# MLP of a two-sample encoder in two passes: Strassen's form in the first layer, the middle kept in DRAM

## The chip, the cores and the metric

The kernel runs on one core of a Trainium2 chip. The metric is device time in microseconds (us), of one execution of the whole program. The engines are PE (TensorE, matrix products into PSUM), DVE (VectorE), ACT (ScalarE), POOL (GpSimd) and SP (SyncE, which issues nearly all transfers).

## What is computed

Two samples of 1024 tokens and 1024 features go through one encoder layer: attention and a state-space mixer side by side, an output projection, an MLP with 4096 hidden columns, and a gate with a side input. The part that the change is about:

```python
    mix = jnp.concatenate([rms_norm(att, g_att_out), rms_norm(ssm, g_ssm_out)], axis=-1)
    h = h + mix @ w_out
    f = rms_norm(h, g_mlp)
    h = h + jnp.square(jax.nn.relu(f @ w_mlp1)) @ w_mlp2
    e = rms_norm(h, g_ple)
    h = h + jax.nn.sigmoid(e @ w_ple_gate) * (p_i @ w_ple_proj)
    ...
    return rms_norm(h, g_final)
```

All of it is fp32. The kernel writes each fp32 operand as a sum of two rounded parts, `hi` and `lo` (a cast on ACT, then a subtraction, "the split"), and a product takes three matmuls: hi·hi, lo·hi and hi·lo (`mm3`, L460 to L463).

## The kernel before

The program has three phases. A (to about 588 us) norms the input, multiplies by `w_in` and runs the state-space part. B (588 to 940 us) is attention together with the gated unit of the mixer (`Glu`, L976); there the order on PE, ACT and DVE is written out by hand in steps, and `GLU_LATE` says how many steps the gated unit starts late. Its tile `yt` is loaded at L1001, squared on POOL (L1005) and taken up by DVE at L1008. C (`PhaseC`, L1149) does the rest, first for sample 0 (943 to 1870 us), then for sample 1 (to 2757 us). In C the order of instructions on each engine is set by a scheduler, which follows the order of the program text where operands and buffers allow and fills gaps with later work.

For one sample C does this. `W_out` is multiplied in two halves of 512 tokens, each added to `h`, which stays in SBUF as eight tiles (L1312). After each half, `norm` makes the normalized rows: squares on ACT, a reciprocal root by Newton's steps on DVE (L419 to L428), a scaled copy `ft` (L556), and per token tile eight transposes on PE into `n_ps` (L561), whose results are split into `acth` and `actl` (L449, L450). Then come eight chunks of 512 hidden columns. Layer 1 of a chunk is a plain product: 4 blocks of 128 columns by 2 token halves by 8 steps of contraction, each three matmuls; POOL splits the weights (L1184), ACT applies relu and square (L1334, L1335), and the tile `hid` stays in SBUF. Layer 2 of the chunk adds `hid` times 512 rows of `w_mlp2` to `h`. It has Strassen's form with seven products p1 to p7 (here run in the order p1, p2, p6, p5, p3, p7, p4): the token halves by the two halves of 256 of the contraction on the left (`hid`), two halves of the contraction by two column halves of 512 on the right (`wr_b`). Sums of the right side are made on POOL (L1217), of the left on DVE (L1222 to L1228), both as 128x1024; each operand is split before its product, the right side on POOL, the left on DVE (both L1184), with three buffers of each kind (`ops`). `into_h` adds the products to `h` (L1270) and to a running sum `u2` (L1279) as they leave PSUM. The last chunk's layer 2 is plain, with the norm for the gate between its halves. The scheduler mixes layer 2 of one chunk with layer 1 of the next on PE. For sample 0, one or two tiles of sample 1's attention output are normed within each chunk (`AttNorm`, L1085), with tiles from the pool `raw`, which also holds layer 1's weights as they land (`w`).

Of the kernel before, what the change touches and what calls it, by code (L numbers as in the profile page):

```python
# [16 lines left out]
P = 128  # L17
# [482 lines left out]
GLU_LATE = 3  # L500
# [475 lines left out]
class Glu:  # L976
# [15 lines left out]
    def gelu(self):  # L992
# [155 lines left out]

class PhaseC:  # L1149
    def __init__(self, nc, tc, ctx, bp, a0, io, ident, scr):  # L1150
        self.nc, self.tc, self.io, self.ident, self.scr = nc, tc, io, ident, scr
        self.bp = bp
# [6 lines left out]
        self.actp = [a0, pool("a", 4)]  # L1159
        self.hp = pool("h", 1)  # L1160
        self.raw = pool("raw", 3)
        self.wp = pool("w", 8)
# [3 lines left out]
        self.pm2 = pool("p2", 5, space=PSUM)  # L1166

# [5 lines left out]
    def norm(self, h, gb, a, i):  # L1173

        a.half(i)
# [11 lines left out]
    def product(self, a, b, ts=range(4)):  # L1187

        nc = self.nc
        banks = {t: self.pm2.tile([P, 512], F32, tag="m2", name="m2") for t in ts}  # L1190
# [15 lines left out]
    def strassen(self, A, s1, B, t2, read, end=(range(4),)):  # L1206

        nc = self.nc
        v, g = nc.vector, nc.gpsimd
# [4 lines left out]
        read(1, self.product([A[0, 0]], B[0, 0]))  # L1218
        each(B[0, 0], B[0, 1], B[0, 0])
        each(t2, B[1, 1], B[0, 0])  # L1220
        read(2, self.product([A[0, 1]], B[1, 0]))
# [357 lines left out]
```

## Time and profile before

| | |
|---|---|
| three runs | 2756.2, 2758.74, 2759.26 us; median 2758.74 |
| the profiled execution | 2758.93 us, with a span of 2757.2 us |
| granted TensorE clock, mean | 0.972 of full speed |
| busy share of the span | PE 93%, DVE 59%, ACT 41%, POOL 41% |

A row of the trace is an instruction, or several alike: start, duration, engine and line, operation, output<-inputs, shapes, and in brackets how long the engine had been idle before it and what released it. Matmuls are pipelined, so a row's duration is longer than the distance to the next one. Windows give the busy time of each engine in a stretch; the stretches used here are the chunks of sample 1 and the layer part of each sample.

### The profile page before, as it was taken

The page shows a single profiled execution, that of the slowest core. Times are in us where ns is not written, and L with a number is a line of the kernel's source. Part 1 is how long each engine was busy: PE and PEld are TensorE (multiplying, and loading weights), DVE is VectorE, ACT ScalarE, POOL GpSimd, SP SyncE. Part 2 cuts the span into 40 slices and gives each one's busy share as a digit, 9 for nine tenths or more (in the row PEclk, how much of TensorE's full clock was granted, in tenths as well). Part 3 has the DMA queues.
Part 4 walks back from the last instruction along what each step waited for, and adds up shares of the span by engine and source line. Part 5 has one row for each costly group of instructions (what it writes and reads, how often), then busy time and mean ns, then how long its engine had stood idle before and what let it go on. Part 6 is the DMA issues. An engine that isn't in the chain of part 4 may idle for free.

```text
span 2757.2 us, 33930 instructions
## 1 busy us (share of the span) xinstructions
PE 2568.5 (93%) x12206; PEld 2040.7 (74%) x12206; DVE 1631.9 (59%) x2891; ACT 1139.8 (41%) x2282; POOL 1138.5 (41%) x819
## 2 busy tenths in 40 slices
PE   5998888969998899999999999999999999999997
PEld 4866666756555677788888878787788888888786
DVE  4788786457766534565555673655355554467455
ACT  6433323327657534333333434443433333333442
POOL 2133234223331243545544653445445555455442
PEclk9999998989999999999999999999999999999999
DMA  8534453355346800221212221262111111111111
GB/s 271 156 85 115 158 177 96 109 162 155 123 135 223 271 31 27 73 73 45 67 46 62 73 88 46 85 224 86 54 54 51 38 58 61 54 54 52 60 39 62
DMA packets 267145, 268.74 MB, mean 97 GB/s; under 512 B 41808, under 2 KB 216912, under 8 KB 264928
## 3 DMA queue, kind: packets, MB, share of 16 engines
q1 hardware_dynamic: 265888, 266.44, 30.5%
q8 instruction: 96, 1.57, 0.2%
q14 instruction: 73, 0.60, 0.1%
q0 software_dynamic: 1088, 0.14, 0.1%
HBM read 196.63 MB, written 67.66 MB: 96 GB/s over the span
## 4 chain that ended last, share of the span: by engine, by line
PE 75%; DVE 14%; DMA 4%; ACT 3%; issue 2%; POOL 1%; SPq 0%; DVEq 0%; ACTq 0%; POOLq 0%
PE m L461 19%; PE m L462 19%; PE m L463 19%; PE ag L462 2%; PE ag L461 2%; PE ag L463 2%; PE glu L1033 2%; PE pss L804 1%; PE pt L844 1%; PE po L865 1%; DMA w<-in_w_mlp_dram 1%; ACT sb L836 1%; PE s_pb L251 1%; PE n_ps L561 1%; DVE s_t L274 1%
## 5 line engine op out<-in xcount | busy, mean ns | idle before, releaser
L1184 POOL TENSOR_TENSOR lo<-wr_b,hi 128x512 fp32r<-128x512 f32 x264 | 381.4, 1452 | 554.1 <-ACT hi L1183 522.7
L461 PE MATMUL m<-acth,hi 128*128 128x512 f32 x1024 | 398.8, 391 | 3.5 <-ACT hi L1183 3.5
L462 PE MATMUL m<-acth,lo 128*128 128x512 f32 x1024 | 399.4, 390 | 1.8 <-POOL lo L1184 1.8
L463 PE MATMUL m<-actl,hi 128*128 128x512 f32 x1024 | 398.4, 390 | 0.0
L1270 DVE TENSOR_TENSOR h<-h,m 128x512 f32<-128x512 f32 x448 | 288.1, 680 | 132.2 <-PE m L463 132.1
L462 PE MATMUL m<-hi,lo 128*128 128x512 f32 x912 | 354.3, 391 | 3.9 <-DVE lo L1184 3.5
L463 PE MATMUL m<-lo,hi 128*128 128x512 f32 x912 | 351.1, 390 | 0.1
L1183 ACT CAST hi<-wr_b 128x512 fp32r<-128x512 f32 x264 | 163.9, 621 | 444.4 <-PE m L462 416.0
L461 PE MATMUL m<-hi 128*128 128x512 f32 x912 | 335.6, 394 | 5.3 <-DVE h L1270 4.1
L1184 DVE TENSOR_TENSOR lo<-hid,hi 128x512 fp32r<-128x512 f32 x200 | 188.2, 942 | 146.3 <-ACT hi L1183 146.2
L1184 POOL TENSOR_TENSOR lo<-w,hi 128x512 fp32r<-128x512 f32 x128 | 176.0, 1382 | 161.4 <-ACT hi L1183 159.1
L461 PEld LDWEIGHTS m<-acth,hi 128*128 128x128 f32 x1024 | 192.3, 188 | 45.2 <-ACT hi L1183 5.1
L462 PEld LDWEIGHTS m<-acth,lo 128*128 128x128 f32 x1024 | 192.7, 188 | 43.7 <-POOL lo L1184 3.9
L463 PEld LDWEIGHTS m<-actl,hi 128*128 128x128 f32 x1024 | 192.4, 188 | 40.2 <-DVE actl L450 0.4
L461 PE MATMUL m<-hi,acth 128*128 128x512 f32 x512 | 201.2, 394 | 5.2 <-DVE h L1312 2.6
L461 PEld LDWEIGHTS m<-hi 128*128 128x128 f32 x912 | 170.9, 188 | 44.3 <-DVE h L1270 7.8
L462 PEld LDWEIGHTS m<-hi,lo 128*128 128x128 f32 x912 | 171.5, 188 | 42.3 <-DVE lo L1184 7.3
L462 PE MATMUL m<-hi,actl 128*128 128x512 f32 x512 | 201.0, 393 | 0.0
L463 PEld LDWEIGHTS m<-lo,hi 128*128 128x128 f32 x912 | 171.5, 188 | 36.4 <-POOL lo L1184 0.9
L463 PE MATMUL m<-lo,acth 128*128 128x512 f32 x512 | 191.3, 393 | 2.3 <-POOL lo L1184 2.3
L1334 ACT ACTIVATE hid<-m 128x512 f32<-128x512 f32 x128 | 76.1, 595 | 218.7 <-PE m L463 217.4
L461 PE MATMUL ag<-acth,whi 128*128 128x512 f32 x384 | 155.3, 406 | 3.6 <-ACT acth L546 3.6
(354 smaller groups left out, 4929.7 us busy)
## 6 DMA issues: line engine op xcount, KB each, us to landing
w<-in_w_mlp_dram SPq DMA_DIRECT2D x128, 256.0 KB, 2.9
wr_b<-in_w_mlp_dram SPq DMA_DIRECT2D x32, 1024.0 KB, 4.9
wraw<-in_w_in_dram SPq DMA_DIRECT2D x32, 512.0 KB, 4.9
out_dram<-h SPq DMA_DIRECT2D x16, 512.0 KB, 2.7
mixa<-ato SPq DMA_DIRECT2D x24, 256.0 KB, 2.5
v<-zv SPq DMA_DIRECT2D x8, 576.0 KB, 6.5
xt<-in_x_sample_dram SPq DMA_DIRECT2D x8, 512.0 KB, 8.2
xt<-in_x_prompt_dram SPq DMA_DIRECT2D x8, 512.0 KB, 5.7
```

The source lines that it names most:

```text
L251: nc.tensor.matmul(pb[:, k], w[:, i, g + k], u[:, g + k], start=True, stop=True)
L274: v.tensor_tensor_scan(flat(dst)[64:128, 0:n - 1][:, ::-1], flat(r0)[64:128, 0:n - 1][:, ::-1], flat(src)[64:128, 1:n][:, ::-1], 0.0, op0= ...
L461: nc.tensor.matmul(out, l[0], r[0], start=first, stop=False)
L462: nc.tensor.matmul(out, l[1], r[0], start=False, stop=False)
L463: nc.tensor.matmul(out, l[0], r[1], start=False, stop=last)
L561: nc.tensor.transpose(pt[:, i], dst[:, P * k:P * k + P], ident)
L804: self.nc.tensor.matmul(pss[h][:, u, w], ql, kr, start=True, stop=True)
L1033: nc.tensor.matmul(o, self.w[:, k, P * f:P * f + P], gt[k][:, c], start=k == 0, stop=k == 3)
L1183: self.nc.scalar.copy(hi, src)
L1184: lo_eng.tensor_tensor(lo, src, hi.bitcast(F32), op=ALU.subtract)
L1270: eng.tensor_tensor(o, o, x, op=ALU.add)
L1334: nc.scalar.activation(z, o, AF.Relu)
```

## The change

Layer 1 gets Strassen's form. A chunk of 512 hidden columns is a 2x2 problem: two halves of 256 hidden columns (weights, left) by two halves of 512 of the contraction by two halves of 512 tokens (right). The seven right sides are three of the normalized quarters, B11, B21 and B22, and four sums T0 to T3. All stay in SBUF, split, for the whole pass: they are made once per sample by the class `Sums`, tile by tile within the norm of the second token half, from the transposes in PSUM and from the first half rebuilt as `f` = hi + lo on POOL. Per token tile DVE makes two differences and the `lo` of two, POOL two differences and the `lo` of two, and ACT five casts. A chunk is then 7 products of 24 matmuls. The results go through relu and square and are stored to DRAM (`hid`); so is `h`, which is loaded again for the second pass.

Layer 2 runs afterwards as a pass of its own: three Strassen groups of 1024 of the contraction (seven products of 48 matmuls, which gather twice the contraction in PSUM), then chunk 6 in the form of 256 and chunk 7 as before. A group loads eight operands of 1 MB into single places. All SBUF of C is divided into 16 places `K(i)`, whose use is rotated from one sample to the next. Operand sums are made in pieces of 128x1024, those of the right side all on POOL (L1264 for both engines), and the products alternate between two PSUM pools. The attention norm of sample 1 moves to chunks 1 to 7 of layer 1. `GLU_LATE` goes from 3 to 5, and the first two loads of `yt` get a higher priority.

The diff, cut to what the prediction speaks of:

```diff
-GLU_LATE = 3
+GLU_LATE = 5
...
-                nc.sync.dma_start(out=yt, in_=scr["y"][8 * f:8 * f + 8, :, :, s].rearrange("g h t c -> (g h) t c"))
+                with B.tc.high_priority(offset=FIRST_AHEAD if s == 0 and f < 2 else 0):
+                    nc.sync.dma_start(out=yt, in_=scr["y"][8 * f:8 * f + 8, :, :, s].rearrange("g h t c -> (g h) t c"))
...
+class Sums:
+    def __init__(self, B, f11, f21, tile, raw):
+        self.B, self.f11, self.f21, self.raw = B, f11, f21, raw
+        self.T = [[tile(i, x) for x in "hl"] for i in range(4)]
+
+    def put(self, nc, kq, T, ps):
+        v, g = nc.vector, nc.gpsimd
+        c = slice(P * (T % 4), P * (T % 4) + P)
+
+        def sum_(i, e, x, y):
+            f = self.raw.tile([P, 4, P], F32, tag="raw", name=f"f{i}")
+            e.tensor_tensor(f, x, y, op=ALU.subtract)
+            hi, lo = (x[:, :, c] for x in self.T[i])
+            nc.scalar.copy(hi, f)
+            e.tensor_tensor(lo, f, hi.bitcast(F32), op=ALU.subtract)
+            return f
+        if kq == 0:
+            self.f1 = sum_(0, v, ps, self.f11[:, :, c])
+            return
+        f2 = sum_(1, v, ps, self.f1)
+        last = self.B.put(nc, kq, T, ps)
+        sum_(2, g, f2, self.f11[:, :, c])
+        sum_(3, g, self.f21[:, :, c], f2)
+        return last
...
-        self.wp = pool("w", 8)
+        self.wp = pool("w", 4)
...
-        def each(out, x, y):
-            for i, (o, p, q) in enumerate(zip(out, x, y)):
-                (v if i else g).tensor_tensor(o, p, q, op=ALU.subtract)
+        def op(e, out, x, y, how=ALU.subtract):
+            for k in range(0, out.shape[1], 2):
+                e.tensor_tensor(*(z[:, k:k + 2] for z in (out, x, y)), op=how)
+        product(1, A[0, 0], B[0, 0])
+        op(g, B[0, 0], B[0, 1], B[0, 0])
+        op(g, t2, B[1, 1], B[0, 0])
+        product(2, A[0, 1], B[1, 0])
+        op(v, s1, A[1, 0], A[1, 1], ALU.add)
+        op(v, A[1, 0], A[0, 0], A[1, 0])
+        op(v, A[0, 0], s1, A[0, 0])
+        op(g, B[0, 1], B[1, 1], B[0, 1])
+        product(6, A[0, 0], t2)
+        op(g, B[1, 0], B[1, 0], t2)
+        op(v, A[0, 1], A[0, 1], A[0, 0])
+        product(5, s1, B[0, 0])
...
+    def layer1(self, ch, o, hid, norm=None):
...
+        def done(i, l, banks, x):
+            z = self.t2.tile([P, 2, 512], F32, tag="t2", name="z")
+            add(z, x, banks)
+            nc.scalar.activation(z, z, AF.Relu)
+            nc.scalar.activation(z, z, AF.Square)
+            nc.sync.dma_start(out=hid[l, :, i], in_=z.rearrange("p f c -> p (f c)"))
...
+        p1 = product(A[0, 0], B11)
+        for f in range(2):
+            nc.scalar.copy(u[:, f], p1[f])
+        done(0, 0, product(A[0, 1], B21), u)
+        if norm:
+            norm()
...
+        f = [K(R[6 + kq], [4, 512], F32, "f") for kq in range(2)]
+        for kq in range(2):
+            nc.gpsimd.tensor_tensor(f[kq], fa.hi[kq, 0].bitcast(F32), fa.lo[kq, 0].bitcast(F32), op=ALU.add)
...
+        for c in range(3):
+            A, b = {}, {}
+            for j, l, pa_, pb_ in ((0, 0, 6, 2), (1, 0, 7, 3), (0, 1, 8, 4), (1, 1, 9, 5)):
+                A[l, j] = K(R[pa_], [4, 512], F32, "hid")
+                nc.sync.dma_start(out=A[l, j].rearrange("p k c -> p (k c)"),
+                                  in_=scr["hid", s, 2 * c + j][l].rearrange("p i c -> p (i c)"))
```

The order that this gives is shown at two places. First POOL, at the start of a layer 2. Before, `wr_b` are operands of `w_mlp2`, `t` is a sum, and `w` are weights of the next chunk's layer 1:

```order
L1184 TENSOR_TENSOR lo<-wr_b_12378,hi 128x512 x2
L1184 TENSOR_TENSOR lo<-wr_b_12380,hi 128x512
L1217 TENSOR_TENSOR wr_b_12378<-wr_b_12378 128x2x512
L1184 TENSOR_TENSOR lo<-w_12312,hi 128x512
L1217 TENSOR_TENSOR t_12382<-wr_b_12380,wr_b_12378 128x1024
L1217 TENSOR_TENSOR wr_b_12378<-wr_b_12380,wr_b_12378 128x2x512
L1184 TENSOR_TENSOR lo<-w_12318,hi 128x512
L1184 TENSOR_TENSOR lo<-wr_b_12380,hi 128x512
L1217 TENSOR_TENSOR wr_b_12380<-wr_b_12380,t_12382 128x2x512
L1184 TENSOR_TENSOR lo<-t_12382,hi 128x512
```

And now, at the start of a group (`wr` are the operands of `w_mlp2`, `t2` the sum):

```order
L1229 TENSOR_TENSOR lo_12132<-wr_12107,hi_12131 128x512
L1229 TENSOR_TENSOR lo_12152<-wr_12107,hi_12151 128x512
L1264 TENSOR_TENSOR wr_12107<-wr_12115,wr_12107 128x1024
L1229 TENSOR_TENSOR lo_12172<-wr_12107,hi_12171 128x512
L1264 TENSOR_TENSOR t2_12122<-wr_12119,wr_12107 128x1024
L1264 TENSOR_TENSOR wr_12115<-wr_12119,wr_12115 128x1024
L1229 TENSOR_TENSOR lo_12192<-wr_12107,hi_12191 128x512
L1229 TENSOR_TENSOR lo_12228<-wr_12111,hi_12227 128x512
L1229 TENSOR_TENSOR lo_12248<-wr_12111,hi_12247 128x512
L1264 TENSOR_TENSOR wr_12107<-wr_12115,wr_12107 128x1024
L1264 TENSOR_TENSOR wr_12111<-wr_12111,t2_12122 128x1024
L1229 TENSOR_TENSOR lo_12268<-wr_12111,hi_12267 128x512
```

Twice as many sums stand between the splits of the first two products, in pieces, and no splits of layer 1 among them. The second place is PE behind `W_out`, in the norm of the second token half. Before (sample 1), `m` here is the first product of layer 2, which runs between the transposes of `n_ps`:

```order
L561 MATMUL n_ps<-ident,ft 128x128 x12
L461 MATMUL m_16229<-hi 128x512
L461 MATMUL m_16230<-hi 128x512
L461 MATMUL m_16231<-hi 128x512
L461 MATMUL m_16232<-hi 128x512
L462 MATMUL m_16229<-hi,lo 128x512
L463 MATMUL m_16229<-lo,hi 128x512
L462 MATMUL m_16230<-hi,lo 128x512
L463 MATMUL m_16230<-lo,hi 128x512
L462 MATMUL m_16231<-hi,lo 128x512
L463 MATMUL m_16231<-lo,hi 128x512
L462 MATMUL m_16232<-hi,lo 128x512
```

After 20 more transposes layer 1 follows there. Now (`mz` are PSUM banks of layer 1, `acth` and `actl` right sides of the first token half, `Th` and `Tl` sums, `B` the quarter B22):

```order
L461 MATMUL mz<-acth,hi 128x512
L462 MATMUL mz<-acth,lo 128x512
L463 MATMUL mz<-actl,hi 128x512
L561 MATMUL n_ps<-ident,ft 128x128 x32
L461 MATMUL mz<-Th,hi 128x512 x4
L461 MATMUL mz<-B_15931,hi 128x512
L462 MATMUL mz<-B_15931,lo 128x512
L461 MATMUL mz<-B_15931,hi 128x512
L462 MATMUL mz<-B_15931,lo 128x512
L462 MATMUL mz<-Th,lo 128x512
```

Ahead of the transposes stand only the rest of the two products that need the first token half alone, and behind them come products that need the second. POOL at the same place (`f` are the rebuilt quarters and the differences):

```order
L1229 TENSOR_TENSOR lo<-w_15941,hi 128x512
L1229 TENSOR_TENSOR lo<-w_15943,hi 128x512
L1438 TENSOR_TENSOR f<-acth,actl 128x2048 x2
L1165 TENSOR_TENSOR f_16077<-f_16071,f 128x512
L1165 TENSOR_TENSOR f_16081<-f,f_16071 128x512
L1168 TENSOR_TENSOR Tl<-f_16077,Th 128x4x128
L1168 TENSOR_TENSOR Tl<-f_16081,Th 128x4x128
L1165 TENSOR_TENSOR f_16106<-f_16100,f 128x512
L1165 TENSOR_TENSOR f_16110<-f,f_16100 128x512
L1168 TENSOR_TENSOR Tl<-f_16106,Th 128x4x128
L1168 TENSOR_TENSOR Tl<-f_16110,Th 128x4x128
L1165 TENSOR_TENSOR f_16135<-f_16129,f 128x512
```

The four operations per token tile stand in tile order, behind the two rebuilt quarters.

## Rows read from the trace of the kernel before

**Rows 1.** Page part 1: engine, busy us (share of the span), instructions

```profile
PE 2568.5 (93%) x12206; PEld 2040.7 (74%) x12206; DVE 1631.9 (59%) x2891; ACT 1139.8 (41%) x2282; POOL 1138.5 (41%) x819
```

**Rows 2.** Windows, one of four: busy us (count) of PE, PEld, DVE, ACT, POOL, clock, DMA share

```profile
2143.20:2224.80 81.60, 81.60 (x362) 67.59 (x360) 43.60 (x59) 30.30 (x53) 41.82 (x27) 1.00 0.17 52
```

**Rows 3.** Windows of the layer part, first and second sample

```profile
1066.60:1755.80 689.20, 675.38 (x2975) 551.18 (x2975) 402.22 (x590) 269.15 (x474) 335.24 (x211) 1.00 0.21 63
1977.60:2643.60 666.00, 663.72 (x2945) 548.57 (x2944) 358.39 (x486) 258.76 (x450) 329.59 (x211) 1.00 0.17 55
```

**Rows 4.** Timeline of PE at 999: start, us, engine, line, operation

```profile
998.77 0.39 PE L462 MATMUL m<-hi,actl 128*128 128x512 f32 x1
...
1000.81 0.39 PE L462 MATMUL m<-hi,actl 128*128 128x512 f32 x1
```

**Rows 5.** Groups by shape, 2143.2 to 2469.6: busy us, mean ns, idle before

```profile
L1184 POOL TENSOR_TENSOR lo<-wr_b,hi 128x512 fp32r<-128x512 f32 x49 | 71.8, 1471 | 97.4 <-ACT hi L1183 94.0 <-DMA wr_b<-in_w_mlp_dram 3.4
...
L1184 DVE TENSOR_TENSOR lo<-hid,hi 128x512 fp32r<-128x512 f32 x48 | 43.5, 905 | 40.0 <-ACT hi L1183 40.0
...
L1279 DVE TENSOR_TENSOR u<-u,m 128x512 f32<-128x512 f32 x32 | 20.7, 676 | 0.0
...
L1217 POOL TENSOR_TENSOR wr_b<-wr_b 128x1024 f32<-128x1024 f32 x4 | 9.6, 2403 | 0.0
...
L1222 DVE TENSOR_TENSOR s<-hid 128x1024 f32<-128x1024 f32 x4 | 5.0, 1260 | 59.0 <-ACT hid L1335 59.0
```

**Rows 6.** Timeline of POOL, 2168 to 2186

```profile
2169.75 1.29 POOL L1184 TENSOR_TENSOR lo<-w,hi 128x512 fp32r<-128x512 f32 x1 [1.43 <-ACT hi L1183]
...
2174.62 2.83 POOL L1217 TENSOR_TENSOR wr_b<-wr_b,t 128x1024 f32<-128x1024 f32 x1
2177.40 2.29 POOL L1184 TENSOR_TENSOR lo<-t,hi 128x512 fp32r<-128x512 f32 x1
```

**Rows 7.** Timeline of DVE, 2168 to 2186

```profile
2174.50 0.68 DVE L1184 TENSOR_TENSOR lo<-hid,hi 128x512 fp32r<-128x512 f32 x1
...
2176.30 2.23 DVE L1224 TENSOR_TENSOR hid<-s,hid 128x1024 f32<-128x1024 f32 x1
```

**Rows 8.** Windows, behind W_out of the second sample

```profile
1951.70:1977.70 26.00, 19.96 (x96) 15.23 (x94) 21.63 (x33) 14.83 (x28) 13.75 (x7) 0.97 0.07 20
```

**Rows 9.** Timeline of PE, first transposes of that norm

```profile
1963.79 1.82 PE L561 MATMUL n_ps<-ident,ft 128*128 128x128 f32 x12 [0.18 <-DVE ft L556]
```

**Rows 10.** Timeline of DVE, 1950 to 1980

```profile
1957.14 2.32 DVE L420 TENSOR_SCALAR nr<-na 128x4 int32<-128x4 int32 x1
...
1962.36 2.48 DVE L556 SCALAR_TENSOR_TENSOR ft<-h,nr,gbc 128x1024 f32<-128x1024 f32 x2
```

**Rows 11.** Timeline of POOL, 1950 to 1980

```profile
1957.03 2.40 POOL L1217 TENSOR_TENSOR wr_b<-wr_b,wr_b 128x1024 f32<-128x1024 f32 x1
```

**Rows 12.** Timeline of PE in attention, 600 to 623

```profile
599.64 1.13 PE L804 MATMUL pss<-k,q 64*128 64x256 f32 x8
...
620.25 1.09 PE L844 MATMUL pt<-ident,sb 128*128 128x128 f32 x4 [18.46 <-DVE pT L848]
```

**Rows 13.** Timeline of PE in attention, 620 to 628

```profile
622.85 2.08 PE L804 MATMUL pss<-k,q 64*128 64x256 f32 x8
```

**Rows 14.** Waits of SP's queue, 938 to 2757: total us, times, longest

```profile
SPq L1100 <- ACT ato L1097: 286.6, 8, 42.8
```

**Rows 15.** Timeline of DVE in attention, 596 to 623

```profile
615.32 2.90 DVE L1008 SCALAR_TENSOR_TENSOR ge<-ge,yt 128x1024 f32<-128x1024 f32 x1 [17.88 <-POOL ge L1005]
```

**Rows 16.** Timeline of POOL in attention, 596 to 623

```profile
613.40 3.74 POOL L1005 TENSOR_TENSOR ge<-yt 128x1024 f32<-128x1024 f32 x2 [34.37 <-DMA yt<-y_scr]
```

**Rows 17.** Timeline of PE at the second sample's start

```profile
1879.89 0.50 PE L461 MATMUL m<-hi,acth 128*128 128x512 f32 x1 [2.60 <-DVE h L1312]
```

**Rows 18.** Page part 6: transfers, count, KB each, us to landing

```profile
wr_b<-in_w_mlp_dram SPq DMA_DIRECT2D x32, 1024.0 KB, 4.9
```

More of the change, by code (lines that the diff above doesn't have):

```diff
@@ L1166, in __init__, with places, tile, half @@
         self.pm2 = pool("p2", 5, space=PSUM)
+        self.R = list(range(16))
+    @staticmethod
+    def places(bp, a0, kp=None):
+        def tile(i, shape, dt, name):
+            pool = a0 if i < 4 else bp if 8 <= i < 12 else kp
+            return pool.tile([P] + shape, dt, tag=f"k{i}", name=name, bufs=1)
+        return tile
+    def half(self, a, th, ids):
+        for kq in range(2):
+            a.hi[kq, th], a.lo[kq, th] = (self.K(i, [4, 512], F32R, "act" + x) for i, x in zip(ids[2 * kq:2 * kq + 2], "hl"))
+        return a
     def gvec(self, src, n):
@@ L1185, in split, with product @@
         return hi, lo
-    def product(self, a, b, ts=range(4)):
+    def product(self, a, b, odd=False):
         nc = self.nc
-        banks = {t: self.pm2.tile([P, 512], F32, tag="m2", name="m2") for t in ts}
+        ts = range(4)
+        banks = {t: (self.pm1 if odd and t < 3 else self.pm2).tile([P, 512], F32, tag="m1" if odd and t < 3 else "m2", name="m2")
+                 for t in ts}
         b = [x[:, k] for x in b for k in range(x.shape[1])]
@@ new lines, in rows, with mixed @@
+    @staticmethod
+    def rows(nc, w, r0, K, i):
+        t = K(i, [2, D], F32, "wr")
+        nc.sync.dma_start(out=t, in_=w[r0:r0 + 2 * P].rearrange("(k p) c -> p k c", p=P))
+        return [t[:, :, 512 * l:512 * l + 512] for l in range(2)]
+    @staticmethod
+    def mixed(nc, K, ids, scr, s, th):
+        A = Act(None, ())
+        for kq, nm in enumerate(("mixa", "ssm")):
+            for i, d in enumerate((A.hi, A.lo)):
+                d[kq, th] = t = K(ids[2 * kq + i], [4, 512], F32R, "mix")
+                nc.sync.dma_start(out=t.bitcast(F32), in_=scr[nm, s][i, :, :, 512 * th:512 * th + 512].rearrange("f p c -> p f c"))
+        A.th = th
+        return A
@@ new lines, in run @@
+                self.norm(h, gb, self.half(fa, 0, R[0:4]), 0)
+        f = [K(R[6 + kq], [4, 512], F32, "f") for kq in range(2)]
+        for kq in range(2):
+            nc.gpsimd.tensor_tensor(f[kq], fa.hi[kq, 0].bitcast(F32), fa.lo[kq, 0].bitcast(F32), op=ALU.add)
+        fa.hi[1, 1], fa.lo[1, 1] = (K(R[4 + i], [4, 512], F32R, "B22") for i in range(2))
+        o = Sums(fa, f[0], f[1], lambda i, x: K(R[8 + 2 * i + "hl".index(x)], [4, 512], F32R, "T" + x), self.raw)
+        for ch in range(8):
+            self.layer1(ch, o, scr["hid", s, ch], None if ch else lambda: self.norm(h, gb, o, 1))
+            if s == 0 and ch > 0:
+                if ch == 1:
+                    N = AttNorm(nc, self.raw, "raw", self.sm, pm1, "m1", ident, self.gvec(io["g_att_out"], 512), io, scr)
+                for T in range(ch - 1, ch + ch // 7):
+                    N.run(1, T, 1)
```

227 lines of the change are left out of this document (119 added, 108 removed).

## The prediction

> **What bounds the kernel now.** I read the busy table first: TensorE works 93% of the span [rows 1]. That is a mean over stages, so the second look is at the stretch that the change rewrites, in windows. Of the second sample's eight chunks, four windows of 81.6 us were taken, and in each of them PE has no idle time at all, while POOL is busy for about half and DVE a little more [rows 2]. The whole layer stretch of that sample is idle on PE for 666.0 - 663.7 = 2.3 us. The first sample's is longer, 689.2 us, with 689.2 - 675.4 = 13.8 us of idle PE [rows 3]. So the MLP is bounded by the number of matmuls, and each matmul removed is worth its own issue time as long as nothing else comes late. A row gives 0.39 us to a 512-wide matmul, but they are pipelined: from 998.77 to 1000.81 there are nine steps, 0.2267 us each [rows 4]. What stands beside PE is read from the shapes in the same stretch [rows 5].
>
> **The matmuls removed.** Layer 1 of one chunk is 4 blocks x 2 token halves x 8 contraction steps x 3 = 192 matmuls now, and 7 products x 24 = 168 in the new form. Layer 2 keeps its count: a group of 1024 is 7 x 48 = 336, and the two chunks that it stands for were 2 x 7 x 24. Saved: 24 x 8 chunks x 2 samples = 384, times 0.2267 = **-87.1 us**. In the order, the 512-wide rows of this arithmetic fall from 9072 to 8688, which is the same 384.
>
> **Layer 1 after.** POOL has 14 splits of 128x512 per chunk where it had 8 and, in layer 2, its sums besides. At the price of an undisturbed one, 1.29 us [rows 6], that is 18.1 us against PE's 168 x 0.2267 = 38.1. DVE has 14 additions with a PSUM operand at 0.68 [rows 5] and four sums at 1.26, 14.6 us in all. Both fit with room, so I cost nothing here; if they did not, each product would wait for its last split.
>
> **The fronts of layer 2.** Before, the additions that make Strassen's operands lie under the next chunk's layer 1, whose 192 matmuls the scheduler mixes in. In the second pass nothing is left to mix in. One contraction step is 12 matmuls, 2.72 us. In a group, the first three products (p1, p2, p6) need nearly all sums: from the first split that three buffers allow, two steps ahead, to the last step of p6 there are 13 steps = 35.4 us. In that time POOL must do 12 splits and 8 sums, 12 x 1.29 + 8 x 2.40 [rows 5, 6] = 34.7 us, which just fits; DVE must do 12 splits at 0.68 [rows 7] and 6 sums at 1.26 [rows 5], 15.7 us. What decides is whether these overlap. In the trace they don't: DVE's L1224 starts at 2176.30 inside POOL's 2.83 us and takes 2.23 instead of 1.26; it ends at 2178.53, just over 1 us after POOL's at 2177.45; POOL's next split, 2177.40, then takes 2.29 instead of 1.29 [rows 5 to 7]. Additions with a PSUM operand stay at 0.68 throughout [rows 5]. Serial work would be 50.4 us; successive starts lie some 0.06 closer than the durations say (2174.62 to 2177.40 is 2.78, the row has 2.83), so with 38 operations about 48, and the group loses 13 us. If POOL alone set the pace it would lose 0. I take 10, nearer the serial end, which is what the rows look like. The first group of a sample can do three sums early, under the last layer-1 chunk, when its weights have landed: 10 - 7 = 3 (bounds 0 and 8). Chunk 6, still of 256, has half the splits and sums: serial 25.2 in 19.0 us, so 6 at most, and I take 4. Per sample 10 + 10 + 3 + 4 = 27, **+54 us** for both, between 0 and 2 x (13 + 13 + 8 + 6) = 80. Behind the front the rest of a group has 16 splits on each engine and two sums on DVE, 34 us of work under 43.5 us of PE, and loses nothing.
>
> The Trainium skill says of this pair (SBUF — State Buffer, "Who interferes with whom") that the port VectorE and GpSimd share is an exclusive lock, not a division of bandwidth. The trace agrees in the 2.23 and 2.29 us just read. Taken strictly it speaks against this change, since it moves all of the right-hand sums to POOL and takes their cover away; the sum by it alone is the first rival's, and by POOL's own time alone the second's.
>
> **The norm of the second token half.** Its matmul stream is thin already: in the 26.0 us behind W_out, PE works 19.96 [rows 8], so 6.0 us are idle. It fills the wait with layer 1 and the first product of layer 2; the first transposes start at 1963.79 [rows 9], 12.1 us after the window's start. Now p1 and p2 of chunk 0 leave 42 matmuls, 9.5 us, and all other products need sums over all four token tiles. Two things are added. First, POOL rebuilds f, twice 128x2048, as soon as W_out has ended; no row shows this shape, I take twice the 2.40 of 128x1024, 4.8 each. Newton's steps on DVE come just then: L420, four columns, took 2.32 under a POOL sum of 2.40 [rows 10, 11]. So the transposes start 0 to 4.4 us later. Second, each tile costs POOL four operations, 5.2 us, and DVE an L556 (1.24 each in the pair of 2.48 [rows 10]) and two splits; serial 7.8 a tile. With three buffers, the next tile's second difference waits for the third of POOL's four. The last T1 part is then ready 4.5 + 2.75 tiles after the first transposes: at 12.1 + 4.5 + 14.3 = 31 or at 16.5 + 4.5 + 21.5 = 42.5 us. PE has 9.5 us of products and some 5 of transposes in it, so it idles 16.5 to 28, less the 6.0 of before: +10.5 to +22. I take +16 per sample, the middle, as f and the lock each may or may not hit: **+32 us**.
>
> **The clock behind a hole.** After 18.46 us without work on PE, eight score matmuls took 2.08 us where the same eight had taken 1.13 just before it [rows 12, 13]: half speed, some 4 us lost. The holes at the norm become longer than 6 us, so I add 2 per sample, **+4** (0 to 8).
>
> **What gets cheaper.** (1) Attention's norm in the first sample shares three raw buffers with the first layer's weights; SP stands 286.6 us at L1100 behind it [rows 14]. The weights get buffers of their own, and of the 13.8 - 2.3 = 11.5 us extra idle PE I take **-9** (0 to -11.5). (2) In attention, DVE waits 17.88 us at L1008 for POOL, POOL for the load of yt [rows 15, 16], and PE 18.46 behind it [rows 12]. The order shows the two loads at the same place on SP as before in spite of the priority, but DVE's operation two steps later, with two score groups and two pT copies ahead of it that used to be behind: **-6** (0 to -12). If the load is what limits, the wait just stays for the later one. (3) At the second sample's start PE waits 2.60 us for an addition to h [rows 17]; h now comes in pairs and earlier, **-2.6** (0 at worst). (4) The additions to h fall to four sevenths, since a group does the work of two chunks; they were under PE, so nothing. Hidden values (32 MB) and h (8 MB) are stored to DRAM and loaded again; 1 MB lands in 4.9 us [rows 18], and a group's 8 MB are spread over 76 us. Nothing in the forecast, but it is a rival.
>
> **Sum**, against the profiled execution's 2758.9 us (the median of the runs shown is 2758.7, the same for this purpose): -87.1 - 9 - 6 - 2.6 + 54 + 32 + 4 = -14.7, so **2744 us**.
>
> **The rivals.** *All port work serial (slower).* Every front pays 13, the first groups 8, chunk 6 pays 6, the norms +22 and 8 for the clock: 80 + 44 + 8 = 132 against 104.7 gained, 2786 us. For it: every overlap in [rows 6, 7] is serial. Against: DVE's sums can slide into gaps when POOL waits for a cast. It decides as soon as fronts, norms and clock pass 110 us together. *POOL alone sets the pace (much faster).* DVE's splits fall between POOL's, fronts cost some 6 per sample, norms +10 each, clock 2: 104.7 - 34 = 71, 2688 us. For it: POOL's own 34.7 us fits in 35.4, and POOL idles half of the layer stretch now [rows 3]. Against: the lock. *The round trip through DRAM comes late.* Each of the eight starts (three groups and chunk 6, two samples) waits one landing of 4.9 for its last operand, since a place is free only when the last product has split it: +40 on the forecast, 2784 us. For it: one place per operand. Against: these places come free three steps before the group ends, and nothing before p2 and the sum s1 needs the last ones. *The load of yt doesn't move*: 2750 us; it is inside the forecast's own range.
>
> **How the numbers follow.** Forecast 0.50, in its own range 2722 to 2766 (about 0.36 faster, 0.11 within, 0.03 slower); serial 0.25, slower; POOL alone 0.15, faster; late loads 0.10, nearly all slower. By over 0.2% (5.5 us, about what a measurement of this kernel can tell from no change): faster 0.52, same 0.12, slower 0.36. The range reaches 2695 to 2790, so that about half of the POOL-alone case and the dearest serial ones stay out.
>
> **What would show it.** In the new profile layer-1 chunks should take 38.1 us of solid PE and middle groups 76.2 plus the front's loss, with PE released by POOL's or DVE's splits in p1 to p6. PE idle in the 30 to 45 us behind W_out should be 16 to 28 us, released by T sums. L1009 on DVE should wait less than 17.9 us. The prediction is wrong in its main step if middle groups run at 76 to 79 us (no lock), or if PE waits there for loads; and in its second if the norm's hole stays near 6 us.

## The result and the profile after

The changed kernel takes 2826.8 us (median of four runs, 2825.7 to 2829.1) against 2758.0: a ratio of 1.0251, with an interval of 1.0233 to 1.0269. It is slower by 69 us, where 15 us less were forecast, and outside the range. The profiled execution has a span of 2824.7 us and a mean granted clock of 0.948 (0.972 before). In the rows of this kernel L461 to L463 are still the three matmuls; a split is L1229, an operand sum of layer 2 L1264, the differences of `Sums` L1165 and their `lo` L1168, the rebuilt `f` L1438, an addition to `h` L1386, and the sums of layer 1's own weights L1361 to L1364.

Page part 1 (engine, busy us, share of the span, instructions), beside [rows 1]:

```profile
PE 2531.4 (90%) x11822; PEld 1996.8 (71%) x11822; DVE 1850.0 (65%) x2963; ACT 1210.5 (43%) x2306; POOL 1357.2 (48%) x951
```

PE has its 384 matmuls less, but only 37 us less of busy time where these matmuls were worth 87, and the span grew by 67.5. So PE idles 105 us more than before, and its mean clock is lower: the time is in PE's waits and in slow matmuls behind them. PE's waits from 930 us to the end (engine, tile, line <- what released it: total us, times, longest):

```profile
PE m L462 <- DVE lo L1229: 73.6, 41, 5.5
PE n_ps L561 <- DVE B L450: 19.7, 4, 5.7
PE mz L461 <- ACT Th L1167: 16.2, 2, 8.1
PE n_ps L561 <- DVE ft L556: 8.3, 4, 3.4
PE m L461 <- DVE h L1386: 7.5, 13, 0.7
PE n_ps L573 <- DVE att L570: 5.4, 1, 5.4
PE n_ps L561 <- DVE f L1165: 5.0, 4, 1.4
```

The first line is layer 2 waiting for a split of a left side; the second, third and seventh are the norm of the second token half; the sixth is the last tile of `AttNorm`. The stages of the second sample, in windows (from:to, length, then busy us and counts of PE, PEld, DVE, ACT, POOL, the clock, DMA share, GB/s): layer 1, the norm ahead of it, the three groups, and the rest to the end.

```profile
2015.80:2311.80 296.00, 296.00 (x1295) 244.87 (x1296) 121.21 (x143) 133.53 (x184) 157.84 (x115) 0.99 0.43 145
1974.30:2015.80 41.50, 17.47 (x76) 13.39 (x74) 34.64 (x44) 19.02 (x35) 30.93 (x15) 0.69 0.20 76
...
2312.00:2403.50 91.50, 81.20 (x335) 65.04 (x334) 73.39 (x68) 37.31 (x63) 63.07 (x37) 0.94 0.35 122
2403.50:2497.20 93.70, 82.32 (x331) 65.76 (x331) 76.57 (x76) 32.49 (x56) 62.12 (x36) 0.93 0.23 84
2497.20:2590.10 92.90, 82.18 (x335) 65.61 (x335) 82.14 (x78) 32.27 (x56) 64.62 (x36) 0.93 0.31 112
2590.10:2824.70 234.60, 210.74 (x932) 169.38 (x930) 160.00 (x253) 92.62 (x166) 114.29 (x75) 0.96 0.09 33
```

Layer 1 is what was forecast: 1296 matmuls without a gap. At the 0.2267 of [rows 4] that is 293.8 us, and it has 296.0. The groups are not: 336 matmuls are 76.2 us at that pace, and the three take 15.3, 17.5 and 16.7 more. Where does one of them lose it? PE in the middle one (start, us, engine, line, ..., in brackets the idle time before and its releaser):

```profile
2409.46 1.07 PE L461 MATMUL m<-hi 128*128 128x512 f32 x4
...
2420.75 2.07 PE L462 MATMUL m<-hi,lo 128*128 128x512 f32 x4 [5.50 <-DVE lo L1229]
2422.63 1.54 PE L463 MATMUL m<-lo,hi 128*128 128x512 f32 x4
2426.82 0.65 PE L462 MATMUL m<-hi,lo 128*128 128x512 f32 x1 [2.65 <-DVE lo L1229]
```

DVE in the same stretch:

```profile
2408.39 2.89 DVE L1229 TENSOR_TENSOR lo<-hid,hi 128x512 fp32r<-128x512 f32 x1
2411.20 3.41 DVE L1264 TENSOR_TENSOR s<-hid 128x1024 f32<-128x1024 f32 x1
2414.53 4.50 DVE L1264 TENSOR_TENSOR hid<-hid 128x1024 f32<-128x1024 f32 x2
2418.95 1.75 DVE L1229 TENSOR_TENSOR lo<-hid,hi 128x512 fp32r<-128x512 f32 x1
2420.62 3.39 DVE L1264 TENSOR_TENSOR hid<-s,hid 128x1024 f32<-128x1024 f32 x1
2423.93 2.83 DVE L1229 TENSOR_TENSOR lo<-hid,hi 128x512 fp32r<-128x512 f32 x1
```

And POOL:

```profile
2407.34 3.39 POOL L1264 TENSOR_TENSOR t<-wr 128x1024 f32<-128x1024 f32 x1
2410.68 2.84 POOL L1264 TENSOR_TENSOR wr<-wr 128x1024 f32<-128x1024 f32 x1
2413.49 6.66 POOL L1229 TENSOR_TENSOR lo<-wr,hi 128x512 fp32r<-128x512 f32 x3
2420.11 2.81 POOL L1264 TENSOR_TENSOR wr<-wr 128x1024 f32<-128x1024 f32 x1
2422.89 3.32 POOL L1264 TENSOR_TENSOR wr<-wr,t 128x1024 f32<-128x1024 f32 x1
```

Read the last two together. Both engines are busy without a pause, and each operation of one lasts until one of the other is through: a sum on DVE is 2.2 to 3.4 us where it was 1.26 alone, a split 1.75 to 2.89 where it was 0.68; POOL's three splits take 6.66 where 3.87 would do. And DVE works in order. PE needs the split that begins at 2418.95; ahead of it stand three sums for later products, from 2411.20 on. PE gets it at 2420.7 and runs the next matmuls at half pace: four in 2.07 us, where four took 1.07 at 2409. The granted clock of that stretch is 0.50, the lower of its two levels (1.2 GHz, where full speed is 2.4):

```profile
2420.70:2423.50 2.80, 2.75 (x7) 2.17 (x8) 2.80 (x1) 0.58 (x1) 2.80 (x2) 0.50 0.00 0
```

Over the three groups of this sample the distances between PE's starts give some 37 us of waits, and some 60 starts that lie 0.42 apart instead of 0.227, 12 us.

The first group has hardly a head start. Its operands are asked for late (SP's queue near the end of layer 1):

```profile
2295.68 0.80 SPq L1460 DMA_DIRECT2D hid<-hid  x2
2301.12 0.93 SPq L1464 DMA_DIRECT2D wr<-in_w_mlp_dram  x2
```

The load of 2301.12 took 8.3 us to land. DVE's first sum starts at 2307.31 and POOL's at 2309.75, with layer 1 done at 2312.0.

In the norm PE idles 41.5 - 17.5 = 24.0 us, at a clock of 0.69, against 6.0 in [rows 8]. From `W_out`'s first half (in the second sample, from behind the wait of [rows 17]) to the 600th matmul of 512 columns behind it, PE takes 19.8 us longer than before, in both samples. POOL's rebuilt `f` and two of its pairs of differences there:

```profile
1974.30 9.18 POOL L1438 TENSOR_TENSOR f<-acth,actl 128x2048 f32<-128x2048 f32 x2 [0.71 <-PE m L462]
1992.14 4.61 POOL L1165 TENSOR_TENSOR f<-f,f 128x512 f32<-128x512 f32 x2 [8.66 <-DVE f L1165]
1996.71 2.50 POOL L1168 TENSOR_TENSOR Tl<-f,Th 128x512 fp32r<-128x512 f32 x2
1999.29 3.80 POOL L1165 TENSOR_TENSOR f<-f,f 128x512 f32<-128x512 f32 x2
2003.05 3.92 POOL L1168 TENSOR_TENSOR Tl<-f,Th 128x512 fp32r<-128x512 f32 x2
```

DVE, which L420 holds up under the first of them, and which has four more operations that the forecast didn't count:

```profile
1978.99 4.52 DVE L420 TENSOR_SCALAR nr<-na 128x4 int32<-128x4 int32 x1
...
1999.68 2.28 DVE L1361 TENSOR_TENSOR s<-w,w 128x1024 f32<-128x1024 f32 x1
...
2004.15 1.69 DVE L1362 TENSOR_TENSOR w<-w,w 128x1024 f32<-128x1024 f32 x1
...
2006.36 1.68 DVE L1363 TENSOR_TENSOR w<-s,w 128x1024 f32<-128x1024 f32 x1
...
2009.17 2.28 DVE L1364 TENSOR_TENSOR w<-w,w 128x1024 f32<-128x1024 f32 x1
```

These are layer 1's weight sums for chunk 0, 7.9 us, put among the differences that PE waits for.

### The profile page after: what moved, and what is told of

Same layout as the page of the kernel before. It is cut to its first block, busy times and chain, and to the rows that moved or that the text cites. A ratio compares the mean times of both kernels' runs of the same rounds, so it can differ in the third digit from the quotient of the medians.

```text
span 2824.7 us, 33883 instructions
## 1 busy us (share of the span) xinstructions
PE 2531.4 (90%) x11822; PEld 1996.8 (71%) x11822; DVE 1850.0 (65%) x2963; ACT 1210.5 (43%) x2306; POOL 1357.2 (48%) x951
## 4 chain that ended last, share of the span: by engine, by line
PE 65%; DVE 24%; issue 4%; ACT 3%; DMA 2%; POOL 2%; SPq 0%; DVEq 0%; ACTq 0%; POOLq 0%
PE m L462 9%; PE m L463 9%; PE m L461 9%; PE mz L461 7%; PE mz L462 7%; PE mz L463 7%; DVE lo L1229 4%; DVE hid L1264 2%; DVE h L1386 2%; PE ag L461 2%; PE ag L462 2%; PE ag L463 2%; PE glu L1034 2%; PE pss L804 1%; PE po L865 1%
## 5 line engine op out<-in xcount | busy, mean ns | idle before, releaser
L1229 POOL TENSOR_TENSOR lo<-wr,hi 128x512 fp32r<-128x512 f32 x328 | 468.5, 1435 | 471.2 <-ACT hi L1228 384.2
L1228 ACT CAST hi<-wr 128x512 fp32r<-128x512 f32 x328 | 203.3, 621 | 542.8 <-PE m L462 459.3
L1229 POOL TENSOR_TENSOR lo<-w,hi 128x512 fp32r<-128x512 f32 x192 | 263.4, 1378 | 240.0 <-ACT hi L1228 228.2
L463 PE MATMUL m<-lo,hi 128*128 128x512 f32 x912 | 336.5, 407 | 0.0
L1229 DVE TENSOR_TENSOR lo<-hid,hi 128x512 fp32r<-128x512 f32 x200 | 256.6, 1299 | 94.4 <-ACT hi L1228 94.2
L461 PE MATMUL m<-hi 128*128 128x512 f32 x912 | 291.0, 404 | 12.5 <-DVE h L1386 7.5
L1228 ACT CAST hi<-w 128x512 fp32r<-128x512 f32 x192 | 117.8, 617 | 238.6 <-PE mz L463 212.9
L461 PEld LDWEIGHTS m<-hi 128*128 128x128 f32 x912 | 176.8, 194 | 57.9 <-DVE h L1386 14.2
L461 PE MATMUL mz<-Th,hi 128*128 128x512 f32 x512 | 200.1, 394 | 16.7 <-ACT Th L1167 16.2
L463 PEld LDWEIGHTS m<-lo,hi 128*128 128x128 f32 x912 | 181.6, 199 | 39.1 <-POOL lo L1229 0.3
L462 PE MATMUL mz<-Th,lo 128*128 128x512 f32 x512 | 200.1, 391 | 0.0
L463 PE MATMUL mz<-Tl,hi 128*128 128x512 f32 x512 | 200.0, 391 | 0.0
L1341 DVE TENSOR_TENSOR z<-u,mz 128x512 f32<-128x512 f32 x128 | 86.6, 683 | 131.9 <-PE mz L463 130.2
L1386 DVE TENSOR_TENSOR h<-h,m 128x512 f32<-128x512 f32 x256 | 158.9, 674 | 3.1 <-PE m L463 3.1
L461 PE MATMUL ag<-acth,whi 128*128 128x512 f32 x384 | 154.6, 404 | 0.9 <-ACT acth L546 0.9
L463 PE MATMUL ag<-actl,whi 128*128 128x512 f32 x384 | 153.3, 404 | 0.0
L462 PE MATMUL ag<-acth,wlo 128*128 128x512 f32 x384 | 152.8, 398 | 0.0
L1341 DVE TENSOR_TENSOR u<-u,mz 128x512 f32<-128x512 f32 x96 | 65.0, 683 | 126.0 <-PE mz L463 126.0
L1228 ACT CAST hi<-hid 128x512 fp32r<-128x512 f32 x200 | 123.5, 617 | 25.1 <-PE m L463 12.8
L461 PEld LDWEIGHTS mz<-Th,hi 128*128 128x128 f32 x512 | 97.2, 190 | 38.0 <-ACT Th L1167 17.0
```

Source lines behind the costliest of these rows:

```text
L461: nc.tensor.matmul(out, l[0], r[0], start=first, stop=False)
L462: nc.tensor.matmul(out, l[1], r[0], start=False, stop=False)
L463: nc.tensor.matmul(out, l[0], r[1], start=False, stop=last)
L1228: self.nc.scalar.copy(hi, src)
L1229: lo_eng.tensor_tensor(lo, src, hi.bitcast(F32), op=ALU.subtract)
L1341: v.tensor_tensor(out[:, f], x[:, f], banks[f], op=ALU.add)
```

## The experiments

My theory after the trace, A in the expectations, is the port: sums of POOL and DVE exclude each other, and what is in the way of a split is the work of both engines together. B puts the loss in DVE's own order, C in late loads; each expectation says what they give. "After" is the changed kernel. Where an interval is given, the time is the median of 4 to 10 runs; `no_pool_sums`, `sums_dve`, `no_sums`, `reorder`, `late`, `late_dve`, `no_T`, `norm_f` and `pre` are one run each. The kernel before, run beside them, had medians of 2757 to 2761 us and single runs up to 12 us apart in one series, so a few us between single runs say nothing. For the experiments on the sums, the time from the first matmul of layer 2 to the end of the program is given for sample 1 (after: 512.7). `no_pool_sums`, `no_sums` and `no_T` leave work out, to measure what it costs.

**The sums of layer 2.** `no_pool_sums` leaves out the four sums of the right side:

```diff
-        op(g, B[0, 0], B[0, 1], B[0, 0])
-        op(g, t2, B[1, 1], B[0, 0])
...
-        op(g, B[0, 1], B[1, 1], B[0, 1])
-        product(6, A[0, 0], t2)
-        op(g, B[1, 0], B[1, 0], t2)
+        product(6, A[0, 0], B[0, 0])
```

> The changed kernel without POOL's sums of the right side in the second pass (so products use unsummed right sides; DVE's sums, all splits and all matmuls stay). Theory A, the shared port: DVE's splits, for which PE waits 73.6 us in layer 2, are late because each of DVE's operations waits for one POOL sum of 2.4 us. Then the groups fall from 93 us to 77 to 80, the clock stays up in them, and the whole is 90 to 120 us faster, 2707 to 2737. Theory B, DVE alone is too slow in its own order (sums ahead of splits): groups stay near 90, 2800 to 2820. Theory C, loads come late: no change, about 2825.

2743.5 us, 83 less than after: somewhat short of A's 90 to 120, far from what B and C give. DVE's own work is the same in this run, but it gets through it faster. In the three groups (line, operands, count, busy us, mean ns; then PE's wait), after and then `no_pool_sums`:

```profile
L1264 DVE TENSOR_TENSOR hid<-hid 128x1024 f32<-128x1024 f32 x13 | 28.4, 2203 | 0.0
PE m L462 <- DVE lo L1229: 28.2, 12, 5.5
```

```profile
L1264 DVE TENSOR_TENSOR hid<-hid 128x1024 f32<-128x1024 f32 x13 | 20.0, 1554 | 0.0
PE m L462 <- DVE lo L1229: 3.8, 4, 2.0
```

A left-side operation of DVE takes nothing from POOL's right side, so what POOL's sums cost it is the time that it is held up. `sums_dve` does the same four on DVE instead (`op(v, ...)` for each `op(g, ...)`):

> The changed kernel with all operand sums of the second pass on DVE, in the changed kernel's own order. Theory A: a sum holds the port for 1.26 instead of 2.40 us, the group's port work falls from 84 to 75 us, and 14 of DVE's operations no longer wait for POOL's longest ones: 20 to 50 us faster than the changed kernel, 2775 to 2805. Theory B, DVE is the engine that is late: eight more sums of 1.26 on it per group, in front of the splits, 7 to 10 us more per group, 2870 to 2890.

2800.1 us, 27 less than after, as A had it, with more work on the engine that PE waits for; the same wait is 14.0 us there. `no_sums` leaves out DVE's four as well:

```diff
-        op(v, s1, A[1, 0], A[1, 1], ALU.add)
-        op(v, A[1, 0], A[0, 0], A[1, 0])
-        op(v, A[0, 0], s1, A[0, 0])
...
-        op(v, A[0, 1], A[0, 1], A[0, 0])
-        product(5, s1, B[0, 0])
+        product(5, A[1, 0], B[0, 0])
```

> The changed kernel without any operand sums in the second pass (POOL's and DVE's left out; splits, matmuls, loads and additions to h stay). If the sums are the whole loss: groups of 76 to 78 us, the first one too, full clock in them, 2705 to 2725. If transfers or the places they go to also cost (late operands at a group's start): groups stay at 80 as without POOL's sums alone, 2735 to 2745.

2708.8 us, where sums as the whole loss gave 2705 to 2725. The windows of the three groups together, and of the rest, in `no_pool_sums`, then `sums_dve`, then `no_sums` (columns as above):

```profile
2270.60:2512.30 241.70, 233.18 (x1004) 188.14 (x1003) 193.56 (x223) 100.43 (x175) 118.81 (x84) 0.99 0.34 121
```

```profile
2302.60:2566.20 263.60, 241.83 (x1009) 194.50 (x1008) 222.80 (x247) 100.31 (x175) 124.74 (x84) 0.95 0.32 115
```

```profile
2252.20:2480.90 228.70, 228.51 (x1008) 188.84 (x1008) 161.21 (x197) 99.33 (x173) 110.71 (x84) 1.00 0.36 130
2480.90:2707.00 226.10, 205.85 (x923) 166.44 (x921) 150.96 (x251) 90.95 (x164) 100.24 (x70) 0.97 0.09 31
```

After has 278.1 for the groups and 234.6 for the rest. Without sums the groups run solid at 76.2 each, full clock. So, by single runs, the operand sums cost 2826.8 - 2708.8 = 118 us: POOL's 83, and DVE's the other 35 when POOL's are gone. Loads from DRAM hold up nothing there, though a group then leaves them 76 us instead of 93. In `sums_dve` 28 operations per sample move from the slower engine to the one that PE waits for, and it saves time: if DVE's own queue were the limit, it would have cost some. With the exclusion it follows, as DVE has to stand through POOL's 2.40 us for a sum that takes 1.26 on DVE itself [rows 5]. The Trainium skill (SBUF — State Buffer, "Who interferes with whom") calls this port an exclusive lock; the alternating rows above agree.

**Order alone.** `reorder` runs p5 before p6 and writes each sum just ahead of the product that needs it:

```diff
         product(1, A[0, 0], B[0, 0])
         op(g, B[0, 0], B[0, 1], B[0, 0])
+        op(v, s1, A[1, 0], A[1, 1], ALU.add)
+        product(2, A[0, 1], B[1, 0])
+        product(5, s1, B[0, 0])
         op(g, t2, B[1, 1], B[0, 0])
```

> The changed kernel with the products of the second pass in the order p1, p2, p5, p6, p3, p7, p4, and each sum emitted just ahead of the product that needs it. All work stays. Theory A: the port has 84 us of work for 76 us of matmuls in a group, but p5 needs only 2 sums of each engine, so less must be done in the first three products; groups of about 84 to 86 us, 40 to 60 us faster than the changed kernel, 2767 to 2787. Theory B, the order on DVE alone: nearly all of the loss goes, groups of 77 to 79, 2725 to 2745. Theory C: no change.

2835.8 us, no gain. Only C had that, and `no_sums` has ruled C out; what happened is that the edit did not move the sums. In the trace the sums stand as far in front as before; the same three of DVE are ahead of a split that PE waits 5.49 us for. Why the scheduler places them there was not looked into. `late` takes that freedom away: same order, and each sum is held behind the last split issued so far.

```diff
+        def after(e, *a):
+            with self.tc.issue_after(self.last[e]):
+                op(*a)
...
-        op(g, B[0, 0], B[0, 1], B[0, 0])
+        after(g, g, B[0, 0], B[0, 1], B[0, 0])
```

> The changed kernel with the products of the second pass in the order p1, p2, p5, p6, p3, p7, p4 and, unlike the run before with that order, each sum really held back on its engine: behind the splits of the product two ahead of the one that needs it. All work and its engines stay. If the loss comes from where the sums stand in front of the splits that PE waits for: a group has 84 us of port work for 76 of matmuls, evenly spread, so 84 to 86 us a group where it is 93; 45 to 65 us faster than the changed kernel, 2762 to 2782. If only the total of the port's work counts, or PE waits for something else: 2820 to 2835, as with the order of products alone.

2826.0 us. A period of 337 matmuls in the middle falls to some 89 us, from 94 to 95 in after, but from the first matmul of layer 2 to the end it has 509.7 against 512.7: the first group gains nothing, and chunk 6, with products half as long, and what follows give back most of what the middle groups gain. Holding sums back in the middle groups alone was not tried. `late_dve` is both, held back and on DVE:

> As the run with sums held back, and all sums on DVE. If the shared port and the order both count: port work 75 us a group, held back sums leave PE no wait of over 1 us at the group's start, groups of 77 to 80 us, 75 to 95 us faster than the changed kernel, 2732 to 2752. If the order does not count: as the run with the sums on DVE in the old order, about 2800.

2797.3 us, 495.5 to the end, the 495.7 of `sums_dve`. So in sum order bought nothing in these runs, and less port work did.

**The norm.** `no_T` leaves out T2 and T3, POOL's four operations per tile (T0 and T1 are used in their place):

```diff
-        sum_(2, g, f2, self.f11[:, :, c])
-        sum_(3, g, self.f21[:, :, c], f2)
```

> The changed kernel without T2 and T3 (POOL's two differences and two lo per token tile, and their casts; layer 1 uses T0 and T1 in their place, all matmuls stay). PE's hole in the norm is 26 us per sample. If POOL's four operations per tile set it: 26 falls to 15 to 18, 2806 to 2812. If DVE's own order (Newton under f, the weights' sums, the splits) sets it: 22 to 25, 2818 to 2825.

2807.4 us, 19 less than after, as expected if POOL's operations set the hole; by the count above 8.7 and 7.3 of it lie in the norms of the two samples. PE's waits in its norm (columns as above):

```profile
PE mz L461 <- ACT hi L1226: 6.5, 1, 6.5
PE n_ps L561 <- DVE B L450: 3.7, 2, 1.9
PE n_ps L561 <- DVE ft L556: 3.4, 1, 3.4
```

The 9.9 us that after waits for L450 in this stretch become 3.7, and its 8.1 for the last T is gone: POOL's chain of four was in the way, for some two fifths of the 19.8. `norm_f` keeps the work but makes chunk 0's weight sums ahead of the norm, and `f` on DVE:

```diff
-            nc.gpsimd.tensor_tensor(f[kq], fa.hi[kq, 0].bitcast(F32), fa.lo[kq, 0].bitcast(F32), op=ALU.add)
+            nc.vector.tensor_tensor(f[kq], fa.hi[kq, 0].bitcast(F32), fa.lo[kq, 0].bitcast(F32), op=ALU.add)
```

> The changed kernel with two edits at the norm of the second token half: layer 1's four sums of weights for chunk 0 are emitted ahead of the norm, and f is rebuilt on DVE. PE's hole there is 26 us per sample; on DVE, L420 stands 4.5 us under POOL's f and the weights' sums take 7.9 us among the differences. If DVE's order sets the hole: 6 to 10 us less per sample, 2807 to 2815. If POOL's four operations per token tile set it: 2 to 4 us per sample, 2819 to 2823.

2815.8 us, 11 less, between the two ranges expected; 2.5 and 3.6 of it lie in the norms, and a single run can't vouch for the rest. `late_dve_norm` joins it to `late_dve`, with a fourth buffer in `raw`:

> The sums held back and on DVE, the two edits at the norm, and a fourth raw buffer for the differences. If layer 2's fronts and the norm are two separate losses, the gains add: 90 to 115 us faster than the changed kernel, 2712 to 2737, which would be faster than the kernel before (2758). If the second pass is bound by something common (transfers, DVE's total), 2760 to 2790.

2783.5 us, 1.0093 of before (1.0076 to 1.0109). That is 14 less than the single run of `late_dve`, so the two gains add; the 2712 to 2737 had counted on a gain of `late_dve` that did not come.

**The loads of yt.** `before_yt` is the kernel before with the change's two edits in attention alone:

```diff
-GLU_LATE = 3
+GLU_LATE = 5
...
+                with B.tc.high_priority(offset=FIRST_AHEAD if s == 0 and f < 2 else 0):
```

> The kernel before, with only the attention part of the change (GLU_LATE 5 and the priority of the first two loads of yt). In the changed kernel the wait of PE in attention fell from 18.46 to 12.75 us, so if that edit stands alone: 5 to 6 us faster than before, about 2753 us. If the two steps of delay cost something later in attention (the gated unit ends later), 0 to 3 us faster.

1.0035 of before (1.0023 to 1.0046): slower, where a gain was expected. PE's waits there, 588 to 960:

```profile
PE pt L844 <- ACT sb L836: 15.9, 2, 13.1
PE px L962 <- DVE ato L1143: 6.8, 3, 5.7
...
PE m L461 <- issue: 4.3, 1, 4.3
```

The wait of [rows 12] is 13.1 instead of 18.46, but new ones of 5.7 and 4.3 stand at the end of attention, where steps that start late have less to hide under, and `W_out` starts at 943.3, as before (943.1). `after_noyt` takes the two edits out of the changed kernel:

> The changed kernel with GLU_LATE 3 and no priority for yt. If the shorter wait in attention counts: 5 to 6 us slower than the changed kernel, 2831 to 2833. If it is given back later in attention, as the run of that edit alone suggests: the same within 3 us, or up to 8 us faster, 2819 to 2829.

2822.6 us, 1.0241 (1.0224 to 1.0258): not apart from after's 1.0251. `W_out` starts at 933.6, in after at 938.1. So the 5 us that after gained there are not from these edits; what they are from stays open.

**A better kernel.** The right side of layer 2 is the same for both samples. `pre` makes its sums once, on POOL under layer 1 of sample 0, stores them, and both samples load them:

```diff
+                    g.tensor_tensor(b00, b01, b00, op=ALU.subtract)
+                    g.tensor_tensor(b01, b11, b01, op=ALU.subtract)
+                    g.tensor_tensor(b11, b11, b00, op=ALU.subtract)
+                    g.tensor_tensor(b10, b10, b11, op=ALU.subtract)
+                    for nm, x in (("b00", b00), ("b01", b01), ("t2", b11), ("b10", b10)):
+                        nc.sync.dma_start(out=scr["bs", c, nm][:, 2 * q:2 * q + 2], in_=x)
```

> The changed kernel, all work kept, with the weights' sums of the three groups made once, in layer 1 of the first sample, by POOL, stored to DRAM, and loaded by both samples' second passes (24 sums of 128x1024 in place of 48, and 3 MB more loaded per group). If POOL's sums cost by holding the port in the second pass: both samples gain what the run without them gained, about 41 us each, less 0 to 10 for layer 1, 2745 to 2757. If the later loads make PE wait, 3 to 5 us a group back: 2765 to 2785. If layer 1 can't hide them either: over 2790.

2775.6 us, 51 less than after, not the 70 to 82 expected: layer 1 of sample 0 became 23 us longer (322.9 against 299.9). `pre_norm` adds the norm's edits and the fourth buffer:

> The same with the two edits at the norm and the fourth raw buffer. The gains should add: 11 us less than the run before, 2732 to 2748, that is 0.4 to 1% faster than the kernel before. If not faster than before, the second pass loses more than POOL's sums.

2757.5 us, 0.9997 of before (0.9988 to 1.0007): 18 less than `pre`, but not the 2732 to 2748 expected. Then four variants. `best1` issues the stores of the sums from POOL's queue and drops the edits of yt; `best2` also holds DVE's sums back as in `late`; `best3` is `best1` with the sums in half pieces in two places; `best4` is `pre_norm` with attention as before and nothing else.

> The run with the weights' sums made once and the norm's edits, with two more: the sums are stored from POOL's queue rather than SP's, and the attention part is as in the kernel before. In that run layer 1 of the first sample lost some 14 us, DVE waiting for weights behind SP's stores of the sums. If that wait is the cause: 12 us and the 4 of the attention part, 2738 to 2746, faster than the kernel before (2757). If it is the port that POOL's extra sums take in layer 1: 2750 to 2756.

> As the run before it, with DVE's sums of the second pass held back behind the splits and p5 ahead of p6. What is left in the groups there is 5 to 6 us each, waits for DVE's splits and for its additions to h. If the order on DVE makes them: 20 to 30 us for both samples, 2710 to 2722. If the order does not count once POOL's sums are gone, or makes other waits: within 5 us of the run before it.

> The weights' sums made once, now in pieces of half the size that alternate between two places, with the sums stored from POOL's queue; the norm's edits; attention as in the kernel before. In the two runs with larger pieces layer 1 of the first sample lost 14 and 24 us, because SP's queue waits for a place before it issues the next weights. If that is so: layer 1 loses 3 to 8 us, 2740 to 2750, faster than the kernel before. If POOL's own stores and the shared port make the loss: 2755 to 2765.

> The run with the weights' sums made once and the norm's edits, larger pieces and stores from SP, with attention as in the kernel before. PE reaches the output projection 5 to 8 us earlier with that attention, so 2749 to 2753, at the edge of faster than before; if that gain is given back in the second phase, the same as before, 2757.

`best1` 2763.0 us, 1.0013 (1.0002 to 1.0024); `best2` 2779.9, 1.0071 (1.0046 to 1.0096); `best3` 2758.4, 0.9983 (0.9970 to 0.9995); `best4` 2755.6, **0.9977 (0.9968 to 0.9986)**. The last beats the kernel before, by 0.2%, as the best of four variants that were tried. `best1` and `best2` missed both ranges of their expectations: with POOL's sums out of the way, holding DVE's back costs 17 us more, and no run says why. In `best4`, layer 2's groups take what they take in `no_pool_sums` (241.7). What it still pays is in layer 1 of sample 0: DVE's longest wait from 980 to 1300, and PE's first there from 950 (L1351 is L1341 of after, L1368 its L1361):

```profile
DVE s L1368 <- DMA w<-in_w_mlp_dram: 29.5, 5, 13.2
```

```profile
PE mz L461 <- DVE u L1351: 11.8, 3, 7.4
```

In after DVE waited 2.9 us for these weights from 980 to 1280. The same wait is 33.0 us in `best1` and 25.1 in `best3`: neither another queue for the stores nor smaller pieces took it away, so what makes the weights late there stays open.

## Why the prediction was wrong

Point by point:

- **Matmuls, -87: right.** 384 fewer, and layer 1 of the second sample at full pace with hardly anything on top (296.0 for 293.8), as forecast. POOL's and DVE's work in layer 1 costs nothing.
- **Fronts of layer 2, +54: the step that failed.** They cost 118 (`no_sums`), 59 per sample, where 27 were forecast; of these sample 1 shows 15.3 + 17.5 + 16.7 in the groups and 234.6 - 226.1 = 8.5 behind them, instead of 3, 10, 10 and 4. The mechanism, work that the port makes serial, was right; its price was not. Three things were too small in it. The middle groups: the bound for serial work, 13, was the right one (some 37 us of waits in three groups), and I took 10, as if part of DVE's work would still fit beside POOL's; the rows above show none that did. The first group: three of POOL's sums in advance were assumed, but the loads are issued too late, POOL has begun one when layer 1 ends, and the group pays nearly what the others pay. And the clock: I had charged half pace for the norm alone, yet the fronts' waits are followed by it too, 12 us in three groups.
- **In-order queues.** The forecast counted how much work must be done before p6 ends, not where in the queue each piece stands. DVE's split for p2 is held by sums for p6. Another place in the queue alone gained nothing in sum (`late`), but the place explains why PE's waits carry DVE's name while POOL's work is the larger cause.
- **Norm, +32 and clock +4: right in mechanism.** The stage, with `W_out`, cost 19.8 per sample, 39.6 in all. `f` took 4.6 (4.8 was estimated) and doubled L420; POOL's chain is some two fifths of the hole (`no_T`). Not foreseen were the weight sums of chunk 0 among DVE's differences.
- **`AttNorm`, -9: half right.** PE no longer waits for it in layer 1, but its last tile stands in the first group, with one wait of 5.4.
- **Second sample's start, -2.6: right.** PE waits for nothing there now.
- **yt, -6: wrong.** The wait shrank by the size forecast, and the end of attention gave it back; alone the two edits cost 0.35%.
- **Rivals.** "All port work serial" had the right direction and mechanism, yet its 2786 was still 41 short, for the clock and the first groups. "POOL alone" falls with the rows of alternating work. "The round trip comes late" falls with `no_sums`, which does the same loads in solid groups.

In sum: -87 + 118 + 40 - 3 is +68, and 69 were measured; the other small terms together are about nothing.

## What to carry to other kernels

When a change takes work away from PE, ask what its cover was for: here 192 matmuls of layer 1 per chunk hid operand sums that cost 118 us once bare. Add the work of two engines that share a port as one serial queue, at the price it has when both are busy, and take the serial end as the forecast if no row shows an overlap. Sums that don't depend on the data are best made once, where matmuls still cover them, and when PE waits for a shared port, less work on it is the thing to try first: here another order gained nothing in sum.

## What the runs showed of the hardware that I had not expected

- A short wait on PE is paid twice. After 5.50 us without work the next matmuls went at some 0.42 us instead of 0.227, at a granted clock of 0.50; some 60 such starts in three groups were 12 us on top of 37 us of waits. The granted clock of the whole groups is 0.93 to 0.94, and 1.00 in the same groups of `no_sums`.
- Size does not protect an operation: L420, on four columns, took 4.52 us under a POOL addition of 128x2048.
- A sum that POOL does in 2.40 us alone costs the pair more than DVE's own 1.26: moving 28 per sample to DVE saved 27 us (one run).
